# A two-layer encoder: the stage of seven products begins two groups earlier

## The chip, the cores and the metric

The kernel runs on one core of a Trainium2 chip. The metric is the time of one execution in microseconds (us) on the device, as the median of repeated runs; a profile was taken of one further execution. The engines are TensorE (PE, its weight loads PEld), VectorE (DVE), ScalarE (ACT), GpSimd (POOL) and SyncE (SP), whose queue issues all the transfers (DMA).

## The reference

Two layers of a streaming encoder over 1152 tokens (1024 of a prompt, 8 x 16 of samples), width 1024. In each layer an attention over a window and a causal convolution work side by side, one output projection joins them, and a feed-forward with a hidden width of 4096 follows. In the code, cut to what matters here:

```python
def finish_layer(x, attn_o, conv_o, beta_a, beta_c, w_out, g2, w_up, w_down):
    x = x + jnp.concatenate([attn_o * beta_a, conv_o * beta_c], axis=-1) @ w_out
    h = rms_norm(x, g2)
    return x + jnp.square(jax.nn.relu(h @ w_up)) @ w_down

for l in range(DEPTH):
    h = rms_norm(yp, norm1_g[l])
    q, k, v, u = project(h, w_in[l], q_norm_g[l], k_norm_g[l], pos_p)
    a_o = band_attention_prompt(q, k, v, attn_sinks[l])
    c_o = conv_tail(jnp.pad(u, ((0, 0), (CONV_STATE, 0), (0, 0))), conv_w[l], conv_b[l], conv_ln_g[l], conv_ln_b[l])
    yp = finish_layer(yp, a_o, c_o, beta_attn[l], beta_conv[l], w_out[l], norm2_g[l], w_up[l], w_down[l])
```

All is float32. The kernel multiplies in parts: each operand is split into a rounded high half and the rest, and three matmuls (high x high, high x rest, rest x high) make one product.

## The kernel before

The tokens lie in three blocks of 384 columns, numbered 0 to 2; the 1024 channels are eight tiles of 128 partitions. One product of a 1024-deep weight tile with a block is 8 x 3 = 24 matmuls of 128x384 (`gemm`, L213 to L215). Weights come as half units of 128x512: SyncE loads `raw`, ScalarE casts the high half into `w` (L205), GpSimd subtracts it for the rest (L206). There are four `raw` buffers (NRAW) and six `w` buffers (NW). Products end in one of three PSUM banks `g` (GB).

The feed-forward is cut into 16 groups of 256 hidden channels. For one block and one group it takes 4 x 12 matmuls up (two column tiles of the hidden layer, L213 to L215, then relu, square and a split by ScalarE and VectorE in `hidden`, L704 to L707) and 8 x 6 matmuls down (`down`, L723, each added to x by VectorE, L725). `feed_one` takes two groups at a time for one block, with 12 matmuls for each down bank. `feed_forward` with two blocks takes one group at a time for both, so that they share the weights.

For the last groups, blocks 0 and 1 go through a stage of seven products (`pair_feed`): a 2x2 partition of weights and activations by Strassen's scheme as Winograd has it, with seven products where eight stand in the plain form. One pass takes two groups: two `pair_up` (7 products of 12 matmuls each, L926) and one `pair_down` (2 x 7 x 12, L1006), 336 matmuls. It needs sums of weights (`S`, VectorE, L879), split by L892 and L893, and sums of the activations (`pair_forms`: differences `t` on GpSimd, L827, sums `m`, `c`, `r` on VectorE, L827, splits by L815 and L816), the last of which overwrite block 1's own `h`. The tiles `S`, `w` and `hid` of this stage lie in a pool `xp` that opens where the pools of the plain form (`hp` for the hidden tiles, `fp`, and the PSUM pool `aux`) close.

Work is interleaved when the program is written. `side` puts a generator on a lane (attention, convolution, forms), and `tick` moves each lane on at its rate; `back` holds one generator of feed-forward work, of which `unit_done` after each product of another stage takes `mix` steps (`fill`), and `flush` takes the rest. A scheduler then orders each engine's instructions by a model of time. `out(b)` is the output projection of block b (`w_out`, additions L695): it finishes the convolution (`tail_of`, whose end is conv_tail: L659, the two steps L249 and L255 of its norm, L670, L673, and L648 and L649, which write `co`), loads x[b] (L190) into one of the nine slots of the pool `big` (NS), and multiplies `ao` and `co` with eight column tiles of w_out.

Per layer: attention and convolution of the three blocks; `out(0)`; block 0's groups 0 to ALONE in the background; `out(1)`; block 1's groups 0 to ALONE; groups ALONE to PLACE for both blocks; then groups PLACE to PAIR for both in the background of `out(2)`; block 2's x is stored (`kept`), and groups PAIR to 16 go through the seven products. Block 2 runs all its groups by itself later.

## Time and profile before

| | |
|---|---|
| runs | 2385.42, 2387.70, 2388.78 us; median 2387.7 us |
| profiled execution | 2387.42 us, its span 2385.6 us |
| TensorE busy | 2312.7 us, 97% |
| VectorE, GpSimd, ScalarE busy | 70%, 63%, 53% |
| mean granted clock of TensorE | 0.995 of full speed |

The span goes from the first to the last instruction in the profile; the time of the execution has 1.8 us more around it. Busy is the share of the span in which an engine had an instruction under way. Matmuls overlap in TensorE's pipeline: one shows as 0.33 us, while the next starts after about half of that. So a busy share of TensorE says little of lost time, and counts of matmuls in a stretch say more.

### The profile page before, as it was taken

What the parts mean: (1) busy time and instruction counts of PE and PEld (TensorE: products, weight loads), DVE (VectorE), ACT (ScalarE), POOL (GpSimd) and SP (SyncE); (2) the same over time, 40 slices, a digit from 0 to 9 for tenths busy, and PEclk for the clock granted to TensorE, in tenths of its full rate; (3) what the DMA queues carried; (4) which work ended last, traced back from release to release, by engine and by line L of the source; (5) the groups of instructions that cost most, each with busy time, mean ns of one, the idle gap of its engine ahead of it and who ended that gap; (6) DMA issues with size and microseconds to landing.
All of it is one profiled execution on the core that took longest, in us unless ns stands there. A gap on an engine that the chain in (4) does not pass through costs nothing.

```text
span 2385.6 us, 39001 instructions
## 1 busy us (share of the span) xinstructions
PE 2312.7 (97%) x13822; PEld 2250.2 (94%) x13822; DVE 1676.6 (70%) x3153; ACT 1269.3 (53%) x2732; POOL 1514.6 (63%) x1247
## 2 busy tenths in 40 slices
PE   7999899999999999999999999999999999999999
PEld 7898898999989999999999999999999899999999
DVE  5999978996378777787687764799834877752222
ACT  5467546555335555644565566466433555544442
POOL 6975485656476665866856866856345666666662
PEclk9999999999999999999999999999999999999999
DMA  5423333434332223443334344434333122254442
GB/s 191 147 88 103 106 111 121 120 121 125 99 96 79 64 71 107 150 135 115 99 119 122 120 142 129 134 99 126 92 106 107 58 71 71 84 164 137 136 126 75
DMA packets 164260, 266.49 MB, mean 112 GB/s; under 512 B 24753, under 2 KB 55729, under 8 KB 164017
## 3 DMA queue, kind: packets, MB, share of 16 engines
q1 hardware_dynamic: 164064, 264.01, 35.8%
q8 instruction: 108, 1.77, 0.3%
q14 instruction: 88, 0.71, 0.1%
HBM read 250.19 MB, written 16.05 MB: 112 GB/s over the span
## 4 chain that ended last, share of the span: by engine, by line
PE 73%; DVE 18%; POOL 4%; issue 3%; DMA 2%; ACT 1%; DVEq 0%; POOLq 0%; SPq 0%; ACTq 0%
PE g L723 13%; PE g L213 12%; PE g L214 12%; PE g L215 12%; DVE c L355 6%; PE x L1006 4%; PE x L926 4%; PE g L1006 3%; PE m L723 2%; PE r L723 2%; PE g L926 2%; POOL w L893 2%; DMA A<-in_w 1%; PE c L723 1%; POOL w L206 1%
## 5 line engine op out<-in xcount | busy, mean ns | idle before, releaser
L206 POOL TENSOR_TENSOR w<-raw,w 128x512 fp32r<-128x512 f32 x728 | 972.7, 1347 | 599.5 <-ACT w L205 589.1
L205 ACT CAST w<-raw 128x512 fp32r<-128x512 f32 x728 | 445.1, 619 | 422.8 <-PE g L215 124.0
L213 PE MATMUL g<-h,w 128*128 128x384 f32 x1696 | 576.4, 341 | 8.2 <-ACT h L284 4.2
L214 PE MATMUL g<-h,w 128*128 128x384 f32 x1696 | 574.1, 339 | 0.6 <-DVE h L285 0.6
L215 PE MATMUL g<-h,w 128*128 128x384 f32 x1696 | 573.1, 338 | 0.0
L355 DVE SCALAR_TENSOR_TENSOR c<-u,vec,c 128x384 f32<-128x384 f32 (+1 forms) x960 | 498.0, 519 | 17.6
L723 PE MATMUL g<-hid,w 128*128 128x384 f32 x2304 | 429.1, 340 | 8.4 <-DVE x L725 5.3
L723 PEld LDWEIGHTS g<-hid,w 128*128 128x128 f32 x2304 | 397.8, 188 | 16.6 <-DVE x L725 9.5
L213 PEld LDWEIGHTS g<-h,w 128*128 128x128 f32 x1696 | 321.0, 189 | 12.4 <-ACT h L284 4.8
L214 PEld LDWEIGHTS g<-h,w 128*128 128x128 f32 x1696 | 321.0, 189 | 2.2 <-DVE h L285 1.0
L215 PEld LDWEIGHTS g<-h,w 128*128 128x128 f32 x1696 | 320.8, 189 | 0.9
L707 DVE TENSOR_TENSOR hid<-t,hid 128x384 fp32r<-128x384 f32 x128 | 107.5, 840 | 186.7 <-ACT hid L706 186.4
L893 POOL TENSOR_TENSOR w<-S,w 128x512 fp32r<-128x512 f32 x96 | 138.6, 1446 | 120.6 <-ACT w L892 120.3
L725 DVE TENSOR_TENSOR x<-x,g 128x384 f32<-128x384 f32 x240 | 130.0, 549 | 66.9 <-PE g L723 66.1
L704 ACT ACTIVATE t<-g 128x384 f32<-128x384 f32 x128 | 62.8, 491 | 148.2 <-PE g L215 147.7
L1006 PE MATMUL x<-F,w 128*128 128x384 f32 x624 | 120.4, 337 | 4.2 <-DVE x L1009 2.3
L893 POOL TENSOR_TENSOR w<-raw,w 128x512 fp32r<-128x512 f32 x64 | 90.5, 1414 | 41.9 <-ACT w L892 40.6
L1006 PEld LDWEIGHTS x<-F,w 128*128 128x128 f32 x624 | 109.3, 188 | 6.0 <-DVE x L947 2.5
L1006 PE MATMUL g<-F,w 128*128 128x384 f32 x528 | 107.6, 339 | 3.3 <-ACT F L815 1.4
L892 ACT CAST w<-S 128x512 fp32r<-128x512 f32 x96 | 59.7, 622 | 93.3 <-DVE S L879 48.2
L1006 PEld LDWEIGHTS g<-F,w 128*128 128x128 f32 x528 | 92.7, 188 | 7.1 <-ACT F L815 2.7
L893 POOL TENSOR_TENSOR w<-A,w 128x512 fp32r<-128x512 f32 x64 | 86.9, 1362 | 19.3 <-ACT w L892 19.1
(237 smaller groups left out, 4010.9 us busy)
## 6 DMA issues: line engine op xcount, KB each, us to landing
raw<-in_w SPq DMA_DIRECT2D x792, 256.0 KB, 2.7
A<-in_w SPq DMA_DIRECT2D x64, 256.0 KB, 2.7
x<-in_x SPq DMA_DIRECT2D x24, 384.0 KB, 5.0
x<-xd SPq DMA_DIRECT2D x12, 384.0 KB, 5.1
kept<-x SPq DMA_DIRECT2D x4, 768.0 KB, 4.0
x<-kept SPq DMA_DIRECT2D x8, 384.0 KB, 4.4
xd<-x SPq DMA_DIRECT2D x4, 768.0 KB, 4.9
out_y<-x SPq DMA_DIRECT2D x4, 768.0 KB, 4.4
```

The costliest lines, as they stand in the source:

```text
L205: nc.scalar.copy(u[:, 0], raw)
L206: nc.gpsimd.tensor_tensor(out=u[:, 1], in0=raw, in1=u[:, 0].bitcast(F32), op=ALU.subtract)
L213: nc.tensor.matmul(ps, lhsT=u(0, k), rhs=h(0, k), start=k == 0, stop=False)
L214: nc.tensor.matmul(ps, lhsT=u(0, k), rhs=h(1, k), start=False, stop=False)
L215: self.pe = nc.tensor.matmul(ps, lhsT=u(1, k), rhs=h(0, k), start=False, stop=k == KT - 1)
L355: t = nc.vector.scalar_tensor_tensor(out=o, in0=src(k), scalar=w, in1=o, op0=ALU.mult, op1=ALU.add)
L707: nc.vector.tensor_tensor(out=hid[:, 1], in0=f, in1=hid[:, 0].bitcast(F32), op=ALU.subtract)
L723: self.pe = nc.tensor.matmul(ps, lhsT=u(p), rhs=hid[:, q], start=i == 0, stop=i == n - 1)
L725: nc.vector.tensor_tensor(out=x[:, m], in0=x[:, m], in1=ps, op=ALU.add)
L893: nc.gpsimd.tensor_tensor(out=u[:, 1], in0=f[n], in1=u[:, 0].bitcast(F32), op=ALU.subtract)
L926: nc.tensor.matmul(ps, lhsT=u[:, p, k], rhs=H[h](q, k), start=start and k == 0 and i == 0, stop=k == 3 and i == 2, skip_group_check=True)
L1006: nc.tensor.matmul(o, lhsT=u[:, p, 2 * i + j], rhs=F(j, hn)[:, q], start=start and n == 0, stop=n == 5, skip_group_check=True)
```

## The change

Three tables are replaced by two. Before, layer 0 had ALONE 6, PLACE 7, PAIR 8, and layer 1 had 4, 6, 8. Now the seven products begin with group 6 in both layers (PAIR), five passes where there were four. Block 0 takes groups 0 to 6 by itself; block 1 takes 0 to 4 (FIRST) by itself and groups 4 and 5 around `out(2)`: its four products up stand ahead of the projection (`self.fill(4)`), its products down are its background. `feed_forward` with its two-block form is gone, and `feed_one` got the argument `then`, called between its last products up and down. FORMS, the rate at which the forms advance with each tick, was 0.3 and 0.2 and is 0.5.

```diff
-ALONE = (6, 4)
-PLACE = (7, 6)
-PAIR = (8, 8)
+PAIR = (6, 6)
+FIRST = (4, 4)
-FORMS = (0.3, 0.2)
+FORMS = 0.5
...
-    def feed_one(self, l, groups, block, pool=None):
+    def feed_one(self, l, groups, block, pool=None, then=None):
...
+            if then is not None and g == groups[-2]:
+                then()
             for m in range(KT):
...
-                self.back, self.mix = self.feed_forward(l, range(alone), [blk(0)]), mix[1]
+                self.back, self.mix = self.feed_one(l, range(pair), blk(0)), mix[1]
...
-                for _ in self.feed_forward(l, range(alone), [blk(1)], True):
-                    pass
-                for _ in self.feed_forward(l, range(alone, place), [blk(0), blk(1)]):
+                for _ in self.feed_one(l, range(first), blk(1)):
                     pass
...
-            self.back, self.mix = self.feed_forward(l, range(place, pair), [blk(b) for b in range(2)], then=firsts), mix[2]
+            self.back, self.mix = self.feed_one(l, range(first, pair), blk(1), then=firsts), mix[2]
+            self.fill(4)
             out(2)
```

Line numbers move: the products down at L723 stand at L722 in the changed kernel, their additions at L724, those of the projection at L694, the conv norm's L255 at L254, the sums `S` at L826, the weights' L206 at L205, and L827 at L774.

The first place is VectorE at the start of the seven products in layer 0. Before (x_4038 is block 1's x, x_7182 that of block 2, S the sums of weights):

```order
L725 TENSOR_TENSOR x_4038<-x_4038,g_7779 128x384
L725 TENSOR_TENSOR x_4038<-x_4038,g_7787 128x384
L725 TENSOR_TENSOR x_4038<-x_4038,g_7795 128x384
L695 TENSOR_TENSOR x_7182<-x_7182,g_7803 128x384
L725 TENSOR_TENSOR x_4038<-x_4038,g_7839 128x384
L725 TENSOR_TENSOR x_4038<-x_4038,g_7847 128x384
L725 TENSOR_TENSOR x_4038<-x_4038,g_7855 128x384
L725 TENSOR_TENSOR x_4038<-x_4038,g_7863 128x384
L879 TENSOR_TENSOR S_7890<-raw_7877,A_7879 128x512
L879 TENSOR_TENSOR S_7892<-S_7890,raw_7873 128x512
```

The same place of the changed kernel (x_6774 is block 2's x):

```order
L694 TENSOR_TENSOR x_6774<-x_6774,g_7069 128x384
L724 TENSOR_TENSOR x_4038<-x_4038,g_7110 128x384
L724 TENSOR_TENSOR x_4038<-x_4038,g_7129 128x384
L826 TENSOR_TENSOR S_7306<-raw_7293,A_7295 128x512
L694 TENSOR_TENSOR x_6774<-x_6774,g_7143 128x384
L826 TENSOR_TENSOR S_7308<-S_7306,raw_7289 128x512
L826 TENSOR_TENSOR raw_7293<-raw_7289,raw_7293 128x512
L826 TENSOR_TENSOR S_7418<-raw_7320,A_7322 128x512
L694 TENSOR_TENSOR x_6774<-x_6774,g_7179 128x384
```

The first sum stood behind the last addition of a product down and all additions of the projection; now four additions of the projection (g_7143, g_7179 and two more) stand behind it.

The second place is TensorE where block 2's convolution ends in layer 0 (r is the bank of the conv norm). Before, products down of block 1's groups 4 and 5 follow:

```order
L723 MATMUL g_6755<-hid_6671,w_6751 128x384 x2
L255 MATMUL r_6617<-cst,s_6625 128x128 x3
L723 MATMUL g_6755<-hid_6671,w_6751 128x384
L723 MATMUL g_6774<-hid_6561,w_6770 128x384 x3
L723 MATMUL g_6774<-hid_6611,w_6770 128x384 x3
L723 MATMUL g_6774<-hid_6671,w_6770 128x384 x3
```

Now (ao is the attention's output, so the last row belongs to the projection's second column tile; the first, g_6779, stands ahead of these rows):

```order
L722 MATMUL g_6856<-hid_6618,w_6852 128x384 x3
L254 MATMUL r_6624<-cst,s_6632 128x128 x3
L722 MATMUL g_6856<-hid_6696,w_6852 128x384 x3
L722 MATMUL g_6875<-hid_6568,w_6871 128x384 x3
L722 MATMUL g_6875<-hid_6618,w_6871 128x384 x3
L722 MATMUL g_6875<-hid_6696,w_6871 128x384 x2
L722 MATMUL g_6856<-hid_6750,w_6852 128x384
L722 MATMUL g_6875<-hid_6696,w_6871 128x384
L722 MATMUL g_6875<-hid_6750,w_6871 128x384
L722 MATMUL g_6856<-hid_6750,w_6852 128x384 x2
L722 MATMUL g_6875<-hid_6750,w_6871 128x384 x2
L212 MATMUL g_6897<-ao_4037,w_6899 128x384
```

Before, 384 more matmuls of groups 6 and 7 and the rest of the downs stood between the norm and most of the projection; now the projection begins around the norm.

The third place is GpSimd in the same stretch of the changed kernel (w are weight halves, t the differences for the forms, s the norm's power):

```order
L230 TENSOR_TENSOR s_6630<-s_6628,half 128x3
L205 TENSOR_TENSOR w_6899<-raw_6898,w_6899 128x512
L774 TENSOR_TENSOR t_6756<-h_5040,h_3255 128x384
L774 TENSOR_TENSOR t_6758<-h_5041,h_3256 128x384
L774 TENSOR_TENSOR t_6815<-h_5040,h_3255 128x384
L774 TENSOR_TENSOR t_6817<-h_5041,h_3256 128x384
L774 TENSOR_TENSOR t_6833<-h_5040,h_3255 128x384
L774 TENSOR_TENSOR t_6835<-h_5041,h_3256 128x384
L774 TENSOR_TENSOR t_6889<-h_5040 128x384
L205 TENSOR_TENSOR w_6904<-raw_6903,w_6904 128x512
L205 TENSOR_TENSOR w_6942<-raw_6941,w_6942 128x512
L774 TENSOR_TENSOR t_6891<-h_5041 128x384
```

The seven differences in a row stood before as well, between other weight halves; now the halves behind them are those of the first two tiles of the projection and of the products down beside them. In layer 1 three more differences follow in the same way.

## Rows read from the trace of the kernel before

**Rows 1.** The page, busy time of each engine.

```profile
PE 2312.7 (97%) x13822; PEld 2250.2 (94%) x13822; DVE 1676.6 (70%) x3153; ACT 1269.3 (53%) x2732; POOL 1514.6 (63%) x1247
```

**Rows 2.** The chain of waits: start us, length us, what.

```profile
609.70 16.66 PE g L723 x96
```

**Rows 3.** Windows: length; busy us and instructions per engine; granted clock; DMA share; GB/s.

```profile
575.30:693.60 118.30, 116.91 (x667) 115.02 (x666) 61.88 (x100) 47.48 (x88) 65.21 (x53) 1.00 0.33 103
693.60:760.80 67.20, 62.13 (x337) 59.53 (x336) 54.91 (x78) 34.57 (x69) 45.37 (x32) 0.97 0.25 79
760.80:823.00 62.20, 59.82 (x339) 58.54 (x338) 46.24 (x74) 32.69 (x65) 39.54 (x29) 1.00 0.22 68
823.00:880.70 57.70, 56.85 (x325) 56.44 (x324) 43.84 (x68) 31.69 (x63) 36.09 (x27) 1.00 0.23 71
...
1722.20:1861.10 138.90, 138.58 (x793) 137.19 (x793) 65.02 (x118) 53.40 (x99) 67.85 (x55) 1.00 0.30 95
1861.10:1925.50 64.40, 58.78 (x324) 56.24 (x325) 54.67 (x76) 34.36 (x69) 44.67 (x32) 1.00 0.24 74
...
1987.80:2045.60 57.80, 56.94 (x326) 56.52 (x326) 43.11 (x68) 31.70 (x63) 36.67 (x27) 1.00 0.24 71
```

**Rows 4.** Waits of TensorE, 693 to 719 us: us, times, longest.

```profile
PE x L926 <- POOL w L893: 1.8, 2, 0.9
PE x L926 <- ACT w L892: 1.7, 1, 1.7
PE x L926 <- DVE t L934: 1.3, 1, 1.3
```

**Rows 5.** Timeline of GpSimd at 700 us: start, length, what, [idle before].

```profile
699.68 1.74 POOL L893 TENSOR_TENSOR w<-S,w 128x512 fp32r<-128x512 f32 x1 [10.72 <-ACT w L892]
```

**Rows 6.** Timeline of VectorE, 697 to 702 us.

```profile
697.79 0.55 DVE L725 TENSOR_TENSOR x<-x,g 128x384 f32<-128x384 f32 x1 [0.49 <-PE g L723]
698.26 0.68 DVE L879 TENSOR_TENSOR S<-raw,A 128x512 f32<-128x512 f32 x1
...
700.19 1.78 DVE L879 TENSOR_TENSOR S<-raw,A 128x512 f32<-128x512 f32 x1
```

**Rows 7.** Timeline of VectorE at 1861 us.

```profile
1860.97 0.55 DVE L725 TENSOR_TENSOR x<-x,g 128x384 f32<-128x384 f32 x1
1861.44 0.69 DVE L879 TENSOR_TENSOR S<-raw,A 128x512 f32<-128x512 f32 x1
```

**Rows 8.** Timelines of TensorE and VectorE, end of the convolution in layer 0.

```profile
578.58 0.49 PE L255 MATMUL r<-cst,s 128*128 128x128 f32 x3
...
588.92 2.76 DVE L649 SCALAR_TENSOR_TENSOR co<-u,vec,co 128x384 fp32r<-128x384 f32 x2
```

**Rows 9.** Loads of x (L190), issue to landing.

```profile
DMA to landing us min/median/max: 3.4/5.0/7.3
```

**Rows 10.** Timeline of SyncE at 606 us.

```profile
605.94 0.90 SPq L190 DMA_DIRECT2D x<-in_x  x2
```

**Rows 11.** Waits of TensorE, 340 to 420 us, the longest.

```profile
PE g L214 <- DVE co L649: 1.4, 1, 1.4
```

**Rows 12.** Groups of GpSimd, 575.3 to 693.6 us: busy us, mean ns | idle before.

```profile
L206 POOL TENSOR_TENSOR w<-raw,w 128x512 fp32r<-128x512 f32 x36 | 48.3, 1356 | 47.2 <-ACT w L205 47.0
L827 POOL TENSOR_TENSOR t<-h 128x384 f32<-128x384 f32 x8 | 8.6, 1098 | 0.0
L827 POOL TENSOR_TENSOR t<-h,h 128x384 f32<-128x384 f32 x8 | 8.2, 1057 | 0.0
```

**Rows 13.** Groups of VectorE in the same stretch.

```profile
L827 DVE TENSOR_TENSOR m<-t,t 128x384 f32<-128x384 f32 x6 | 6.8, 1140 | 2.8 <-POOL t L827 2.8
...
L816 DVE TENSOR_TENSOR T<-m,T 128x384 fp32r<-128x384 f32 x4 | 2.2, 549 | 0.5 <-ACT T L815 0.5
```

**Rows 14.** A window in the same stretch, columns as in rows 3.

```profile
660.00:680.00 20.00, 18.61 (x102) 17.12 (x101) 18.36 (x32) 8.34 (x17) 20.00 (x18) 1.00 0.27 80
```

**Rows 15.** Waits of TensorE, 575 to 694 us, the longest.

```profile
PE g L723 <- DVE x L695: 0.9, 1, 0.9
```

More of the change, by code (lines that the diff above doesn't have):

```diff
@@ L754, in feed_one @@
                     yield
-    def feed_forward(self, l, groups, blocks, lag=False, pool=None, then=None):
-        a = self.a
-        if len(blocks) == 1:
-            yield from self.feed_one(l, groups, blocks[0], pool)
-            return
-        hids, ups, downs = {}, {}, {}
-        def up(e):
-            g, b = e
-            hids[e] = []
-            for j in range(2):
-                if (g, j) not in ups:
-                    ups[g, j] = self.unit(a["w"][l, 22 + 2 * g + j])
-                ps, _ = self.pg()
-                self.mark = self.gemm(ps, ups[g, j], blocks[b][1])
-                hids[e].append(self.hidden(ps))
-                self.tick()
-                yield
-        def down(e):
-            g, b = e
-            hid = hids.pop(e)
-            for j in range(2):
-                if (g, j) not in downs:
-                    downs[g, j] = self.unit(self.w_down(l, g)[:, ROW[g % 2 * 2 + j]::4], pool)
-            for m in range(KT):
-                self.down(blocks[b][0], m, [(lambda p, j=j: downs[g, j](p, m), hid[j]) for j in range(2)], pool)
-                if m % 4 == 3:
-                    if g == groups[-1]:
-                        self.stored(blocks[b], m, 4)
-                    self.tick()
-                    yield
-        es = [(g, b) for g in groups for b in range(len(blocks))]
-        if lag:
-            prev = None
-            for e in es:
-                yield from up(e)
-                if prev is not None:
-                    yield from down(prev)
-                prev = e
-            yield from down(prev)
-        else:
-            n = len(blocks)
-            for i in range(0, len(es), n):
-                for e in es[i:i + n]:
-                    yield from up(e)
-                if then is not None and i == len(es) - n:
-                    then()
-                for e in es[i:i + n]:
-                    yield from down(e)
     def parted(self, f, dst):
@@ L1041, in run @@
             nh = []
-            alone, pair, place, mix, conv, att = (t[l] for t in (ALONE, PAIR, PLACE, MIX, CONV, ATT))
+            pair, first, mix, conv, att = (t[l] for t in (PAIR, FIRST, MIX, CONV, ATT))
             def blk(b, end=False, x=x, h=h, nsrc=nsrc, nh=nh, l=l, fin=fin):
@@ L1098, in run @@
             forms, three, fourth = self.pair_forms(h[0], h[1])
-            self.side("forms", three, FORMS[l])
+            self.side("forms", three, FORMS)
             def firsts(l=l, fourth=fourth):
@@ L1141, in run @@
                 with tc.tile_pool(name=f"fp{l}", bufs=NFW) as fp:
-                    for _ in self.feed_forward(l, range(NG), [blk(2, True)], True, fp):
+                    for _ in self.feed_one(l, range(NG), blk(2, True), fp):
                         pass
             else:
-                self.back = self.feed_forward(l, range(NG), [blk(2, True)])
+                self.back = self.feed_one(l, range(NG), blk(2, True))
                 self.fill(FILL)
```

## The prediction

> **What bounds the kernel now.** The page comes first: TensorE is busy for 97% of the span, VectorE for 70%, GpSimd for 63% [rows 1]. So TensorE is the limit, and what remains to be found is the number of its matmuls and the places where it stands still. The chain of waits gives the price of a matmul: 96 in a row of the down product take 16.66 us, 0.1735 us each [rows 2]. Every matmul that the change touches has this form (128x384), so time lost in a stretch is its length less its count times 0.1735.
>
> The windows by stage [rows 3] then show three kinds of stretch. In the two from the last products up of block 1's first groups to the start of the seven products ("transition" from here on), 118.3 us hold 667 matmuls (115.7 us) in layer 0, and 138.9 us hold 793 (137.6 us) in layer 1: 2.6 and 1.3 us are lost. The first pass of the seven products takes 67.2 us for 337 matmuls and 64.4 us for 324: 8.7 and 8.2 us lost. The second and third passes take 62.2 us for 339 and 57.7 us for 325, so 3.4 and 1.2 us are lost, and in layer 1 the last row shows 57.8 us for 326, 1.2 us lost again. A pass counts 336 in the code; a window counts those that cross its edge twice.
>
> The wait view of the first pass says why it is dear [rows 4]: TensorE waits for weights from ScalarE and GpSimd (1.7 and 1.8 us), then for VectorE. Going back: GpSimd's first product weight that needs a sum begins at 699.68 us, after 10.72 us of idleness that ScalarE's cast ended [rows 5]; the cast waited for the sum; and VectorE made that sum at 698.26 us, directly behind the addition of the very last product down, at 697.79 us [rows 6]. Layer 1 repeats it: addition at 1860.97, first sum at 1861.44 us [rows 7]. In code the reason is plain: sums and weights of the stage lie in pool xp, which opens where the pool of the hidden tiles closes, so the last product down must have read them.
>
> **The change, part by part.**
>
> *Matmuls.* In each layer two groups of two blocks leave the plain form (2 blocks x 2 groups x 96 = 384 matmuls) and enter the seven products (336). That is 96 fewer in all: 96 x 0.1735 = 16.7 us off. They leave stretches in which TensorE is full, so this comes off the end.
>
> *One more pass per layer.* A pass loses between 1.2 and 3.4 us beyond its matmuls. In TensorE's order pass 3 of the changed kernel is interleaved exactly as pass 3 of before, passes 2 and 4 most nearly as pass 2, the dearer. So I take 3.4 us for the added one, 6.8 us in both layers (bounds 2.4 and 6.8).
>
> *The start of the seven products.* Now the last product down stands in front of four whole column tiles of the out projection: 4 x 24 x 0.1735 = 16.7 us. In VectorE's order the first sums come ahead of the additions of these four, so sums, casts and the weights that GpSimd splits have 16.7 us in which they cost nothing. The first pass should then lose what a later one loses, between 1.2 and 3.4, say 2.4 us: 8.7 + 8.2 - 4.8 = 12.1 us off. Bounds: nothing gained, if another wait takes the place of the sum, and 14.5 us, if both first passes fall to 1.2. If the cover were gone (the raw weights late behind the store of the third block, which heads SyncE's queue), the 12.1 us stay lost.
>
> *The transition, layer 0.* The out projection now begins only some ten products after the convolution's last step, and this has a price. From TensorE's broadcast (L255, 578.58 us) to VectorE's last split of co (591.68 us) the trace shows 13.1 us [rows 8]. The nine slots of the big pool (NS) are all taken, and the third block's x gets the one that the convolution's input gives up when co is done, so its load comes behind that: its landing takes 3.4 us at best and 5.0 us in the median [rows 9]; then 0.55 us for the addition. That frees the first bank 17.1 to 18.7 us after L255. The order puts 78 matmuls (6 + 12 + 12 + 12 + 24 + 12) between L255 and the product that needs that bank: 13.5 us. TensorE stands still for 3.6 to 5.2 us, part of it earlier on co itself. Before, the same load was issued at 605.94 us [rows 10], with plain products as cover. I take 4.6 us lost instead of 2.6: +2.0 us. The nearest case, out projection 1 of layer 0, where co is also just in time, shows a wait of 1.4 us for co [rows 11], which speaks for the lower end.
>
> *The transition, layer 1.* Here co is ready before the products up, and GpSimd is the risk. Ten differences for the sums of h stand with three weight halves in a row in its queue; at 1.08 and 1.36 us [rows 12] that is 14.9 us. GpSimd can be six weight tiles ahead (NW = 6, 12 matmuls each): 12.5 us. The rest, some 2.4 us, shows up on TensorE; what was lost before is partly the same kind. I take 2.8 us for 1.3: +1.5 us. Bounds: below, nothing lost in either transition (-3.9 us together); above, 5.2 us in layer 0, and in layer 1, if GpSimd has no lead at all when the differences begin, 14.9 less the 6.2 us that three halves give TensorE, 8.7 us.
>
> *Weights without sharing.* Block 0's and block 1's groups in layer 1 now load and split their own weights: 32 halves per two groups and two blocks where it was 16. A half gives TensorE 12 x 0.1735 = 2.08 us of work and costs GpSimd 1.36 us, so splitting hides; 0 us. The larger additions per bank (12 matmuls instead of 6) spare VectorE work off the path: 0 us.
>
> *Sum*, against the profiled execution's own 2387.42 us (the median of the runs shown is 2387.7, 0.3 above): -16.7 + 6.8 - 12.1 + 2.0 + 1.5 = -18.5, so 2368.9 us; as a median, 2369 us.
>
> One rule speaks against this. In rows 6 the same sum S<-raw,A takes 0.68 us at 698.26 and 1.78 us at 700.19 us, when GpSimd is splitting weights. The Trainium skill (SBUF — State Buffer, section Who interferes with whom) says that a VectorE instruction with two SBUF inputs and a GpSimd instruction that reads SBUF exclude each other, and that the later one waits for the whole of the other; the trace agrees with it in that row. By it the two engines' times in the transition would add up rather than overlap, which makes the slower rival below likelier than the sum alone does.
>
> **The rivals.**
>
> *The start stays dear* (12%). The sums are early, but a tile or a load is not: the first pass still loses 8 us. For it: SyncE's queue is in order, and a store of x stands before the last raw tiles. Against it: each of these loads has over 10 us before it is used. Sum: 2369 + 12.1 = 2381 us.
>
> *GpSimd and VectorE take turns* (5%); this one ends slower. In one transition GpSimd has 32 halves x 1.356 and 16 differences (8.2 + 8.6 us): 60.2 us [rows 12], against 384 x 0.1735 = 66.6 us of TensorE, where before it had 118 us. VectorE's part of the sums of h is 8 sums of two differences at 1.14 us [rows 13] and 32 operations at 0.55: 26.7 us. If these never overlap, a transition lasts 86.9 us, 20.3 more than TensorE needs; over both layers, less the 3.5 us allowed for, 2369 + 37 = 2406 us. It decides once more than some 15 us are lost in each transition. For it: GpSimd was full for 20.00 of 20 us in 660 to 680 us [rows 14]. Against it: there VectorE was busy for 18.36 of the same 20, and TensorE waited for VectorE only 0.9 us at its longest in the whole stretch [rows 15].
>
> *Half of that* (6%): 8 to 9 us lost more in each transition, 2386 us, no change to be seen.
>
> *Better than the sum* (10%): both first passes fall to 1.2 us, the added pass costs 1.2, the transitions lose nothing: -16.7 + 2.4 - 14.5 - 3.9 = -32.7; halfway there is 2362 us.
>
> **How the numbers follow.** The forecast has the remaining 67%: 2369 us, between 2364 (the first passes and layer 0's transition at their lower ends) and 2375 (both transitions at their upper bounds). The range 2361 to 2381 takes in the first rival and half of the last. Some 0.2% (4.8 us) is what a measurement of this kernel tells from no change. Forecast, better sum and first rival lie below 2382.9 us, the last of them narrowly: faster 0.88, the same 0.07, slower 0.05.
>
> **What would show it.** Five passes a layer, the middle three at 58 to 62 us. In the first pass, no granted clock below 1.00 (0.97 now [rows 3]) and its length near 60 us. The first sum S<-raw,A earlier than the last addition of the out projection. In layer 0's transition, waits for VectorE's co and for x, 4 to 5 us together, and in layer 1's, short waits for GpSimd's weights. I am wrong if the first pass keeps waits for GpSimd's product weights of microseconds, or if a transition loses more than 8 us.

## The result, and the profile after

The median of the changed kernel is 2374.3 us (2372.5 to 2378.0, four runs) against 2387.8 us: ratio 0.995, 95% interval 0.9934 to 0.9965. It is 13.5 us faster (8 to 16 by the interval), where 18.5 were forecast. The profiled execution took 2373.73 us, its span is 2371.7 us.

The first part of the page, to be read against [rows 1]: 96 matmuls fewer, and VectorE and GpSimd busier.

```profile
PE 2296.1 (97%) x13726; PEld 2235.5 (94%) x13726; DVE 1719.8 (73%) x3201; ACT 1300.9 (55%) x2796; POOL 1571.5 (66%) x1287
```

Next the windows by stage (length, busy us and instructions of PE, PEld, DVE, ACT, POOL, granted clock, DMA share, GB/s). All cuts from here on are at the same events in every kernel: the *plain stretch* runs from the last matmul of the third block's attention to the first of the seven products, and behind it comes the first pass. Nearly all matmuls there are 128x384, so that the loss is again the length less the count times 0.1735 us; the cuts make it uncertain by some 0.5 us. First before (its plain stretches reach further back than the transitions in [rows 3]):

```profile
523.00:693.60 170.60, 169.21 (x968) 166.78 (x968) 102.61 (x184) 75.08 (x144) 97.80 (x77) 1.00 0.37 115
1690.80:1861.10 170.30, 169.98 (x976) 168.28 (x975) 89.01 (x167) 66.54 (x128) 75.28 (x61) 1.00 0.29 93
```

The changed kernel, in layer 0 the plain stretch and the first four passes, in layer 1 the plain stretch and the first pass:

```profile
523.80:633.50 109.70, 106.06 (x595) 104.76 (x594) 86.65 (x150) 55.25 (x108) 84.98 (x65) 0.97 0.42 140
633.50:692.10 58.60, 55.53 (x315) 54.16 (x313) 44.30 (x67) 31.31 (x63) 37.02 (x28) 1.00 0.27 89
692.10:756.20 64.10, 61.83 (x350) 60.55 (x350) 47.85 (x78) 33.38 (x66) 39.86 (x29) 1.00 0.22 68
756.20:813.90 57.70, 56.85 (x325) 56.44 (x324) 43.89 (x68) 31.71 (x63) 36.29 (x27) 1.00 0.23 71
813.90:876.70 62.80, 61.52 (x350) 60.56 (x349) 47.46 (x76) 33.23 (x66) 39.43 (x29) 1.00 0.21 70
...
1685.00:1791.90 106.90, 103.97 (x595) 102.09 (x594) 75.03 (x118) 55.80 (x108) 83.75 (x65) 1.00 0.44 143
1791.90:1848.90 57.00, 55.10 (x314) 54.25 (x313) 42.52 (x67) 31.43 (x63) 36.08 (x27) 1.00 0.28 91
```

The first passes lose 3.9 and 2.5 us where they lost 8.7 and 8.2 [rows 3]. The plain stretches lose 109.7 - 595 x 0.1735 = 6.5 us and 3.7 us, where they lost 2.7 and 1.0. So the start gave 10.5 us, and more than half of that (6.5 us) was lost ahead of it. The waits of TensorE say on whom (us in total, times, longest); in the plain stretch of layer 0, of layer 1, and in layer 0's first pass:

```profile
PE g L212 <- DVE x L724: 2.2, 1, 2.2
PE g L722 <- DVE hid L706: 1.4, 1, 1.4
...
PE g L722 <- POOL w L205: 1.8, 1, 1.8
PE g L214 <- POOL w L205: 0.8, 1, 0.8
...
PE x L873 <- DVE t L881: 1.2, 1, 1.2
PE g L873 <- ACT t L877: 1.1, 1, 1.1
PE x L953 <- DVE x L956: 0.8, 1, 0.8
```

In the first pass, GpSimd's product weights, which cost 1.8 us before [rows 4], are gone from the list. In layer 1's plain stretch GpSimd's weights are there, as forecast. In layer 0's it is neither co nor the load of x, but a split of the hidden tile and an addition on VectorE. The timelines at that place, of GpSimd and of VectorE (start, us, instruction, idle time before it and its releaser):

```profile
579.20 6.46 POOL L774 TENSOR_TENSOR t<-h,h 128x384 f32<-128x384 f32 x6
...
581.21 1.37 DVE L774 TENSOR_TENSOR m<-t,t 128x384 f32<-128x384 f32 x1 [2.43 <-POOL t L774]
582.49 1.34 DVE L706 TENSOR_TENSOR hid<-t,hid 128x384 fp32r<-128x384 f32 x1
583.76 0.55 DVE L763 TENSOR_TENSOR T<-m,T 128x384 fp32r<-128x384 f32 x1
584.22 1.74 DVE L669 TENSOR_TENSOR u<-u,r 128x1536 f32<-128x1536 f32 x1
586.00 0.56 DVE L774 TENSOR_TENSOR r<-h,c 128x384 f32<-128x384 f32 x1
586.47 0.55 DVE L724 TENSOR_TENSOR x<-x,g 128x384 f32<-128x384 f32 x1
```

VectorE stands 2.43 us at a sum m whose differences GpSimd makes in a run of six; the hidden tile's split comes behind it, and the addition behind that, the convolution's L669 and more sums. TensorE waited 1.4 us for the split, until 583.9 us, and 2.2 us for the addition (the one at 586.47 us, which ends at 587.0, and TensorE goes on at 587.1). So the activations' sums are a suspect, and with them the weights that GpSimd splits for each block apart.

### The profile page after: what moved, and what is told of

It reads as the page before. It is cut to its first block, busy times and chain, and to the rows that moved or that the text cites. A ratio compares the mean times of both kernels' runs of the same rounds, so it can differ in the third digit from the quotient of the medians.

```text
span 2371.7 us, 39078 instructions
## 1 busy us (share of the span) xinstructions
PE 2296.1 (97%) x13726; PEld 2235.5 (94%) x13726; DVE 1719.8 (73%) x3201; ACT 1300.9 (55%) x2796; POOL 1571.5 (66%) x1287
## 5 line engine op out<-in xcount | busy, mean ns | idle before, releaser
L205 POOL TENSOR_TENSOR w<-raw,w 128x512 fp32r<-128x512 f32 x712 | 954.6, 1353 | 506.6 <-ACT w L204 495.2
L212 PE MATMUL g<-h,w 128*128 128x384 f32 x1568 | 532.1, 340 | 7.9 <-ACT h L283 3.9
L213 PE MATMUL g<-h,w 128*128 128x384 f32 x1568 | 530.1, 338 | 0.6 <-DVE h L284 0.6
L214 PE MATMUL g<-h,w 128*128 128x384 f32 x1568 | 529.1, 338 | 0.0
L722 PE MATMUL g<-hid,w 128*128 128x384 f32 x1920 | 363.6, 342 | 9.2 <-DVE x L724 4.1
L722 PEld LDWEIGHTS g<-hid,w 128*128 128x128 f32 x1920 | 333.5, 189 | 16.3 <-DVE x L724 5.4
L212 PEld LDWEIGHTS g<-h,w 128*128 128x128 f32 x1568 | 295.8, 189 | 12.3 <-ACT h L283 4.7
L213 PEld LDWEIGHTS g<-h,w 128*128 128x128 f32 x1568 | 296.0, 189 | 2.3 <-DVE h L284 1.0
L214 PEld LDWEIGHTS g<-h,w 128*128 128x128 f32 x1568 | 295.8, 189 | 0.9
L840 POOL TENSOR_TENSOR w<-S,w 128x512 fp32r<-128x512 f32 x120 | 168.8, 1409 | 129.1 <-ACT w L839 126.9
L953 PE MATMUL x<-F,w 128*128 128x384 f32 x780 | 151.2, 337 | 5.3 <-DVE x L956 3.4
L953 PEld LDWEIGHTS x<-F,w 128*128 128x128 f32 x780 | 136.8, 188 | 7.2 <-DVE x L956 4.7
L953 PE MATMUL g<-F,w 128*128 128x384 f32 x660 | 133.7, 338 | 0.9 <-DVE x L894 0.4
L953 PEld LDWEIGHTS g<-F,w 128*128 128x128 f32 x660 | 115.9, 188 | 3.8 <-DVE x L894 2.0
L956 DVE TENSOR_TENSOR x<-x,x 128x384 f32<-128x384 f32 x160 | 83.8, 545 | 47.7 <-PE x L953 47.2
```

Of the source, the lines that this page charges most:

```text
L205: nc.gpsimd.tensor_tensor(out=u[:, 1], in0=raw, in1=u[:, 0].bitcast(F32), op=ALU.subtract)
L212: nc.tensor.matmul(ps, lhsT=u(0, k), rhs=h(0, k), start=k == 0, stop=False)
L213: nc.tensor.matmul(ps, lhsT=u(0, k), rhs=h(1, k), start=False, stop=False)
L214: self.pe = nc.tensor.matmul(ps, lhsT=u(1, k), rhs=h(0, k), start=False, stop=k == KT - 1)
L722: self.pe = nc.tensor.matmul(ps, lhsT=u(p), rhs=hid[:, q], start=i == 0, stop=i == n - 1)
L840: nc.gpsimd.tensor_tensor(out=u[:, 1], in0=f[n], in1=u[:, 0].bitcast(F32), op=ALU.subtract)
```

## The experiments

**Theory A:** the start of the seven products is dear or cheap by where the last products down stand, and nothing else in the change touches it. The shortfall comes from GpSimd's and VectorE's work for the sums of the activations and for unshared weights, which lies beside fewer products than before. **Rivals:** the start is cheaper for another reason; the shortfall is the end of the convolution and the load of x (the forecast's own account), or only the order of the sums.

All losses below are worked out as above (us):

| kernel | median us | plain, layer 0 | first pass | plain, layer 1 | first pass |
|---|---|---|---|---|---|
| before | 2387.8 | 2.7 | 8.7 | 1.0 | 8.2 |
| changed | 2374.3 | 6.5 | 3.9 | 3.7 | 2.5 |
| e1, no early products up | 2392.0 | 9.0 | 6.8 | 8.5 | 8.3 |
| e2, before with early products | 2375.9 | 1.8 | 1.2 | 1.6 | 4.5 |
| e3, changed with four passes | 2381.5 | 4.1 | 3.8 | 3.9 | 2.1 |
| e4, convolution earlier | 2371.1 | 6.8 | 2.5 | 3.7 | 2.3 |
| e5, no sums of activations | 2362.7 | 0.7 | 1.1 | -0.5 | 1.7 |
| e6, differences on VectorE | 2380.7 | 11.8 | 2.1 | 4.2 | 2.1 |
| e7, e4 and sums spread | 2371.6 | 7.1 | 2.4 | 5.6 | 1.2 |
| e8, e4 and products down first | 2372.1 | 6.0 | 2.6 | 6.7 | 1.3 |
| e9, e4 and sums earlier | 2369.8 | 6.1 | 1.0 | 5.7 | 2.1 |
| e12, shared weights, five passes | 2375.1 | 7.1 | 1.3 | 2.2 | 1.4 |

**e1.** The products up run no longer ahead of the projection:

```diff
-            self.fill(4)
             out(2)
```

> The changed kernel without the early run of four products up: groups 4 and 5 of block 1 are interleaved with the third block's projection again, so the last product down ends right ahead of the seven products. Theory A (the start is cheap because four bare column tiles of the projection stand between the last product down and the first product of the seven): the first passes lose 8 to 9 us again instead of 4.0 and 2.5, +4.5 and +6; layer 0's transition has the products up as cover for the third block's x and gives back 2 to 4 of its 6.4 us. Together +6.5 to +10.5: 2381 to 2385 us, first passes of about 63 us in both layers. Rival B (the first passes are cheaper for another reason, the shorter plain stretch or the unshared weights, not for the place of the last products down): they stay at 57 to 58.6 us, and the time is 2370 to 2375 us.

It took 2392.0 us (2389.2 to 2396.5), ratio to before 1.002 (1.0011 to 1.0029): 17.7 us more than the changed kernel. In the windows the first passes are dear again, and the plain stretches lose more as well:

```profile
524.10:636.50 112.40, 105.36 (x596) 103.85 (x595) 78.80 (x145) 53.27 (x104) 76.08 (x61) 0.97 0.43 141
636.50:699.70 63.20, 58.58 (x325) 56.11 (x324) 53.73 (x76) 34.45 (x69) 45.36 (x32) 1.00 0.24 76
1691.70:1803.40 111.70, 105.83 (x595) 103.62 (x595) 74.33 (x116) 54.77 (x108) 78.99 (x63) 0.98 0.42 136
1803.40:1866.20 62.80, 56.04 (x314) 54.06 (x313) 48.37 (x69) 31.32 (x63) 41.35 (x30) 1.00 0.27 85
```

Theory A holds for the start (8.7 us more in the two first passes), and was wrong in that the plain stretch would be eased. The waits of layer 0's plain stretch tell why there:

```profile
PE g L212 <- ACT co L647: 4.9, 1, 4.9
PE r L254 <- DVE s L242: 2.2, 1, 2.2
```

The early products up cover the steps of the convolution's norm too. Without them co is waited for, 4.9 us, and the norm 2.2 us. (In layer 1 the longest wait is 2.8 us, for an addition on VectorE.) Without its one line the change would have been no gain.

**e2.** The kernel before, with one line more:

```diff
+            self.fill(8 if l else 4)
             out(2)
```

> The kernel before (seven products from group 8, four passes) with the products up, and in layer 0 the first down, of block 1's last groups run ahead of the third block's projection, so that bare column tiles of the projection stand ahead of the first pass. Theory A: the first pass of layer 0 falls from 67.2 us (8.7 lost) to about 61 (2.4 to 4 lost), 5 to 6 us off; in layer 1 the last product down still stands 12 matmuls ahead of the start, so there 0 to 2 us come off; the transition of layer 0 loses up to 2 us more. Together 2380 to 2384 us. Rival B (the place of the last products down is not what made the start dear): no difference, 2387 to 2389 us, first pass of layer 0 at 66 to 67 us.

It took 2375.9 us (2375.3 to 2376.5), ratio 0.995 (0.9939 to 0.9962). That is 11.9 us off, from the order alone, with the old number of matmuls:

```profile
523.60:695.40 171.80, 171.10 (x980) 168.90 (x979) 108.65 (x192) 77.36 (x149) 104.62 (x81) 1.00 0.35 114
695.40:751.10 55.70, 54.85 (x314) 54.28 (x313) 40.45 (x66) 31.33 (x63) 36.02 (x27) 1.00 0.28 93
1683.20:1847.90 164.70, 163.51 (x940) 162.14 (x940) 91.28 (x163) 66.00 (x128) 75.19 (x61) 1.00 0.29 92
1847.90:1915.20 67.30, 64.08 (x362) 62.64 (x361) 54.44 (x79) 34.27 (x69) 45.35 (x32) 1.00 0.26 83
```

Layer 0's first pass loses 1.2 instead of 8.7 us, layer 1's 4.5 instead of 8.2, and the plain stretches lose no more than before. That the start is cheaper for another reason than the place of the products is refuted; what I had expected of it (2380 us at best) was too little in both layers.

**e3.** The changed kernel with four passes:

```diff
-PAIR = (6, 6)
-FIRST = (4, 4)
+PAIR = (8, 8)
+FIRST = (6, 6)
```

> The changed kernel with four passes instead of five: seven products from group 8, block 1's groups 6 and 7 around the third block's projection, in the same order as the changed kernel has 4 and 5. Theory A (a pass more costs what the middle passes lose): 96 matmuls more (+16.7 us), one pass less per layer (-2.1 -2.3 to -3.4 -3.5), and layer 0's transition, where the convolution's end is then two groups further ahead of the projection, gives back 2 to 4 of its 6.4 us: +6 to +10, 2380 to 2384 us. Rival B (the matmuls taken out were not on the path, and all of the gain is the start of the seven products): 2372 to 2376 us, as the changed kernel. Rival C (the stall of layer 0's transition is not the convolution's end): no relief there, 6.4 us lost again, 2384 to 2387 us.

It took 2381.5 us (2380.2 to 2384.5), ratio 0.9977 (0.9968 to 0.9985): the fifth pass is worth 7.2 us, as theory A said. Set beside e2 it tells more. Both have 13822 matmuls, four passes and products ahead of the projection; e3 goes block by block and splits each weight twice. It differs in two more ways: its sums go at rate 0.5, and in layer 1 it has only the products up ahead of the projection, where e2 has the whole of group 6. It is 5.6 us slower. Its plain stretches of both layers, and the waits in either of them:

```profile
521.50:695.50 174.00, 171.63 (x979) 168.75 (x978) 104.42 (x175) 86.15 (x164) 126.37 (x97) 1.00 0.42 137
1687.00:1860.60 173.60, 171.23 (x978) 168.62 (x977) 89.42 (x143) 85.57 (x164) 125.03 (x97) 1.00 0.41 137
```

```profile
PE g L722 <- POOL w L205: 1.0, 2, 0.5
PE g L214 <- POOL w L205: 0.8, 1, 0.8
```

GpSimd is busy for 126 and 125 us, where e2's row shows 105 and 75, and TensorE waits 1.8 us in each layer for its weights (e2 waits for none in layer 0, and 1.2 us in layer 1). The losses there are 4.1 and 3.9 us against 1.8 and 1.6. With the first pass counted in, though, layer 1 loses 6.0 us in e3 and 6.1 in e2, and the whole difference lies in layer 0: 7.9 against 3.0.

**e4.** The third block's convolution in layer 0 a step faster:

```diff
-CONV = ((6, 5, 3), (3.5, 3.5, 3.5))
+CONV = ((6, 5, 4), (3.5, 3.5, 3.5))
```

> The changed kernel with the convolution of the third block in layer 0 moved on at a rate of 4 instead of 3, so that its last steps end earlier, ahead of the transition; layer 1 is as it was. Theory A (TensorE's 6.4 us in layer 0's transition are lost because the convolution's end, the forms' differences and the last products up fall together on VectorE and GpSimd): the transition loses 2 to 3.5 us, and the spell at half clock there is gone: 2370 to 2372 us. Rival B (the forms alone make the stall, a run of ten differences on GpSimd with VectorE's sums behind them): it stays at 5 to 7 us, 2373 to 2376 us.

It took 2371.1 us, ratio 0.9928 (0.9917 to 0.994, where the changed kernel's interval begins at 0.9934). The gain is not where theory A put it: the plain stretch of layer 0 loses 6.8 us, as much as before the edit. Rival B is right about the place and wrong about the time, since the gain lies ahead. The windows up to the plain stretch, of the changed kernel and of this one (its profiled execution was the fastest of its runs):

```profile
0.00:523.80 523.80, 483.98 (x3046) 459.70 (x3046) 463.21 (x979) 311.67 (x744) 346.87 (x317) 0.98 0.37 122
```

```profile
0.00:518.00 518.00, 481.93 (x3046) 459.19 (x3046) 457.97 (x977) 311.41 (x744) 347.25 (x317) 0.98 0.38 123
```

The same 3046 matmuls end 5.8 us earlier, beside the attention. But the run does not test the convolution's end: the projection came forward with it. From the norm's last step on TensorE (L254) to the first matmul on co there are 9.3 us in e4 and 14.4 in the changed kernel. Its place is tested by e5 and e8.

**e5.** The sums of the activations are left out; the seven products read h in their place.

```diff
-                "T1": part(T1), "T2": part(T2), "T4": part(T4)}, three(), fourth()
+                "T1": h1, "T2": lambda p, k: h1(p, 4 + k), "T4": h0}, iter(()), iter(())
```

> The changed kernel without the sums of the activations: the differences on GpSimd, the sums, splits and casts on VectorE and ScalarE are left out, and the seven products read plain halves of h in their place (so the output is not the reference's; TensorE's matmuls are the same). Theory A (the transitions lose what they lose because of these sums: VectorE in layer 0, GpSimd's queue in layer 1): layer 0's transition falls from 6.4 us lost to 1 to 3, layer 1's from 3.8 to 1 to 2, and the half-clock spell in layer 0's transition is gone; 2374 less 5 to 8 is 2366 to 2369 us. Rival B (the losses come from the convolution's end, the products up and the load of x, whatever the sums do): the transitions stay within 1 us of 6.4 and 3.8 us, 2372 to 2375 us.

```profile
531.90:635.80 103.90, 103.55 (x595) 102.34 (x595) 65.43 (x113) 49.97 (x94) 66.61 (x50) 1.00 0.42 137
1681.50:1784.10 102.60, 102.60 (x594) 102.30 (x593) 52.82 (x79) 49.50 (x94) 66.90 (x50) 1.00 0.42 139
```

Both plain stretches are full: 0.7 us lost and none, at full clock, though in layer 0 the convolution's end (8.4 us from the norm's last step to the first matmul on co) and the load of x are still there, and in both layers the weights without sharing. So without the sums nothing else in the stretch stalls TensorE. The median, 2362.7 us, is not a clean price, because the kernel without the sums' tiles differs elsewhere too (its first 300 us hold 1649 matmuls, the changed kernel's 1700); only these windows are used. Nor does e5 say what the convolution's end costs beside the sums, since it has no sums. The same groups of VectorE by form show how the sums act on what stands beside them, the split of the hidden tile in the plain stretch of layer 0, with the sums (changed) and without (e5):

```profile
L706 DVE TENSOR_TENSOR hid<-t,hid 128x384 fp32r<-128x384 f32 x8 | 7.2, 901 | 2.1 <-ACT hid L705 2.1
```

```profile
L706 DVE TENSOR_TENSOR hid<-t,hid 128x384 fp32r<-128x384 f32 x8 | 5.6, 702 | 2.5 <-ACT hid L705 2.5
```

One takes 901 ns with GpSimd busy for 85.0 us of the stretch, 702 ns with 66.6. The Trainium skill (SBUF — State Buffer, Who interferes with whom) has VectorE instructions with two inputs in SBUF, as this split is, and GpSimd's reads of SBUF exclude each other; the rows agree in direction.

**e6.** The 16 differences of a layer on VectorE:

```diff
-            d = op(nc.gpsimd, self.tmp(), F(h1, 0, k), F(h, 0, j), sub)
-            e = op(nc.gpsimd, self.tmp(), F(h1, 1, k), F(h, 1, j), sub)
+            d = op(nc.vector, self.tmp(), F(h1, 0, k), F(h, 0, j), sub)
+            e = op(nc.vector, self.tmp(), F(h1, 1, k), F(h, 1, j), sub)
```

> The changed kernel with the differences for the sums of the activations (16 in each layer) on VectorE instead of GpSimd. Theory A (in layer 1 GpSimd's queue is what TensorE waits for, in layer 0 VectorE's, which stands behind GpSimd's differences): layer 1's transition falls from 3.8 us lost to 1.5 to 2.5 and shows no wait for GpSimd's weights; in layer 0 VectorE gets 10 to 16 operations of 0.55 to 1.1 us more but no longer waits 2.4 us for GpSimd, so 5 to 8 us are lost there. Together 2371 to 2376 us. Rival B (VectorE is the tight one in both): both transitions lose 2 to 5 us more, 2378 to 2384 us.

It took 2380.7 us (2375.1 to 2381.9), ratio 0.9965 (0.9952 to 0.9977). The plain stretch of layer 0:

```profile
524.90:639.90 115.00, 107.04 (x595) 104.60 (x594) 98.00 (x168) 55.34 (x109) 68.22 (x49) 0.97 0.41 133
```

In layer 0 the loss goes from 6.5 to 11.8 us: VectorE is the tight one there, busy for 98 of 115 us. In layer 1 it stays at 4.2, but no wait for GpSimd's weights is left; the longest are now for an addition on VectorE (1.3 us) and for a cast on ScalarE (1.2 us). Neither theory was right in whole: the time is rival B's, layer 1 lies between the two.

**e7, e8, e9.** Three other orders, each on top of e4. The sums spread over the products up:

```diff
-FORMS = 0.5
+FORMS = 1
```

> The changed kernel with the third block's convolution at rate 4 in layer 0 and the sums of the activations moved on at rate 1 instead of 0.5 with each product, so that they are spread over the four products up and do not come in one run behind the last of them; it is to be compared with the kernel that has the convolution's rate alone (2371.1 us). Theory A (the run of sums in one piece makes the stalls in both layers): layer 0's transition loses 2 to 4 us, layer 1's 1.5 to 3; 2365 to 2369 us. Rival B (it is their amount against 66.6 us of products, not where they stand): within 2 us of 2371.

Two steps of products down, too, ahead of the projection:

```diff
-            self.fill(4)
+            self.fill(6)
```

> The changed kernel with the third block's convolution at rate 4 in layer 0 and two steps more of block 1's products down (of the four in a transition) ahead of the third block's projection, so that six instead of four of its column tiles stand bare ahead of the seven products; to be compared with the kernel that has the convolution's rate alone (2371.1 us). Theory A (what stalls in layer 0 is the first tiles of the projection, behind the convolution's end and the load of x; the products down ahead of it are cover): layer 0's transition falls from some 6 us lost to 3 to 5, the first passes stay within 1 us; 2367 to 2371 us. Rival B (the additions of the products down stand in VectorE's queue behind the sums, wherever the projection stands): the transition loses as much or up to 3 us more; 2371 to 2375 us.

The sums begun two groups of block 1 earlier:

```diff
-FIRST = (4, 4)
+FIRST = (2, 2)
...
-            self.fill(4)
+            self.fill(12)
```

> The changed kernel with the third block's convolution at rate 4 in layer 0, and with the sums of the activations begun one stretch of two groups earlier in both layers: eight of a layer's 16 differences then lie beside block 1's groups 2 and 3 and only the other eight beside the transition; TensorE's order is nearly that of the kernel with the convolution's rate alone (2371.1 us), to which it is to be compared. Theory A (it is the amount of sums beside the 66.6 us of the transition's products that stalls, on GpSimd and with it on VectorE): the transitions lose 2 to 4 us less in each layer, and the half-clock spell in layer 0's is gone: 2363 to 2368 us. Rival B (the sums stall TensorE wherever they stand, since their operations hold VectorE and GpSimd in turn; the loss moves to block 1's groups 2 and 3): 2370 to 2373 us. Rival C (what remains in layer 0 is the convolution's end and the load of x): layer 1 gains 2 to 3 us, layer 0 nothing: 2368 to 2370 us.

They took 2371.6, 2372.1 and 2369.8 us (intervals 0.9921 to 0.9944, 0.9922 to 0.9946 and 0.9908 to 0.9935). None can be told from e4, so rival B holds in e7 and e8. In e8 the projection begins 9.1 us behind the norm's last step, where it begins 3.1 us ahead of it in the changed kernel, and layer 0 still loses 6.0 us: a projection too near to the convolution's end is not the main cause. The time of e9 lies between rivals B and C; by the place it is B, since layer 1 gains nothing (5.7 us lost, 3.7 in e4). TensorE's longest wait in layer 0's plain stretch now ends at 546.1 us, in the groups ahead of the transition:

```profile
PE g L722 <- DVE x L724: 1.8, 1, 1.8
```

The plain stretches lose 6.1 and 5.7 us with half the sums some 33 us earlier: what the transition gained, the groups ahead of it lost. Over e4 and these three, layer 0 loses 6.0 to 7.1 us and layer 1 3.7 to 6.7, wherever the sums stand.

**e10, e11.** A sixth pass, in layer 1 alone (with the early sums in layer 0), and in both layers:

```diff
-PAIR = (6, 6)
-FIRST = (4, 4)
+PAIR = (6, 4)
+FIRST = (2, 2)
...
-            self.fill(4)
+            self.fill(4 if l else 12)
```

> The kernel with the sums begun earlier in layer 0 (as the one before), and in layer 1 the seven products from group 4 instead of 6, so one pass more there (48 matmuls fewer, 8.3 us), with the sums beside the transition. Theory A (a further pass pays its matmuls less 2.5 to 3.5 us, as the fifth did): 5 us off the layer; against it, the attention of the third block now has two groups of products fewer beside it, 1 to 4 us lost: within -5 to +1 of the kernel with the early sums, less the 2 to 3 us that early sums give in layer 1, so 2363 to 2370 us. Rival B (attention, convolution and sums no longer fit beside what is left of the products): 2372 to 2380 us.

```diff
-PAIR = (6, 6)
-FIRST = (4, 4)
+PAIR = (4, 4)
+FIRST = (2, 2)
...
-CONV = ((6, 5, 3), (3.5, 3.5, 3.5))
+CONV = ((6, 5, 6), (3.5, 3.5, 3.5))
```

> The changed kernel with the seven products from group 4 in both layers, six passes instead of five (96 matmuls fewer, 16.7 us), the third block's convolution in layer 0 at rate 6 so that it ends in time, and the sums beside the transition. Theory A (each pass more pays 8.3 us of matmuls less 2.5 to 3.5): 10 us less than the 2371 to 2374 us of the changed kernel, less 2 to 6 us of losses because the attention, the convolution and the sums have fewer products beside them: 2364 to 2370 us. Rival B (these no longer fit): losses of 10 us or more in each layer, 2375 to 2385 us.

They took 2399.3 and 2457.8 us (ratios 1.0047, 1.0034 to 1.0059, and 1.0292, 1.0278 to 1.0306): both misses, rival B in kind and worse in size. Layer 1's plain stretch in e10, its longest waits, and the place in layer 0 of e11 where the convolution is finished:

```profile
1672.90:1759.50 86.60, 59.26 (x301) 56.18 (x302) 62.74 (x117) 31.47 (x61) 41.23 (x32) 0.81 0.29 98
...
PE r L658 <- DVE T L763: 10.5, 1, 10.5
PE g L212 <- ACT co L647: 6.2, 1, 6.2
PE r L248 <- DVE f L665: 5.1, 1, 5.1
```

```profile
510.00:578.00 68.00, 18.52 (x65) 14.97 (x66) 43.70 (x102) 18.89 (x56) 9.27 (x12) 0.50 0.10 35
...
PE r L658 <- DVE f L655: 34.7, 1, 34.7
```

34 us are lost in e10 (86.6 - 301 x 0.1735): the convolution's end and its norm wait for VectorE with nothing beside them. A part of the first wait is of another kind: L658's operand was ready at 1697.4 us, but it writes the bank r, of which the kernel has one at this place, and a sum of the activations held that until VectorE had split it at 1704.7 us. The plain products are the cover for the third block's attention and convolution, and the seven products, which come behind, can't be. As these stages stand, with that one bank for both, neither try at a sixth pass paid; a second bank was not tried.

**e12.** Five passes in the form of before, where blocks 0 and 1 share the weights of the last plain groups:

```diff
-ALONE = (6, 4)
-PLACE = (7, 6)
-PAIR = (8, 8)
+ALONE = (4, 4)
+PLACE = (5, 5)
+PAIR = (6, 6)
...
-FORMS = (0.3, 0.2)
+FORMS = (0.5, 0.5)
...
+            self.fill(4)
             out(2)
```

> The kernel before with the seven products from group 6 in both layers (five passes, as many matmuls as the changed kernel), the products up of blocks 0 and 1 for group 5 ahead of the third block's projection, and the sums of the activations at rate 0.5; so it differs from the changed kernel in that both blocks go through their last plain groups together and share these weights (block 0 has four groups by itself instead of six). Theory A (the weights without sharing, costed at nothing, are a price: with four passes the form by blocks lost 5.6 us against the shared form, 2381.5 to 2375.9): half the groups' weight splits leave GpSimd's queue in the transition, which loses 2 to 3 us less in each layer; 2367 to 2371 us. Rival B (sharing is worth nothing here, and those 5.6 us were the rate of the sums or the place of the projection): 2373 to 2377 us. Rival C (block 0's two groups less beside the third block's attention leave that stage uncovered in layer 1): a loss of 3 to 10 us ahead of the transition there, 2374 to 2382 us.

It took 2375.1 us (2372.5 to 2377.6), ratio 0.9951 (0.9938 to 0.9965): the changed kernel's time, rival B's. The windows say it is not that sharing is worth nothing. Up to layer 0's plain stretch, and the two plain stretches:

```profile
0.00:517.70 517.70, 479.21 (x2990) 453.93 (x2991) 455.72 (x963) 309.01 (x740) 338.61 (x311) 0.97 0.37 120
517.70:637.70 120.00, 116.45 (x651) 112.90 (x651) 99.43 (x183) 49.66 (x99) 69.78 (x56) 0.99 0.33 106
1687.20:1792.10 104.90, 104.08 (x592) 101.68 (x592) 76.07 (x133) 47.05 (x93) 62.04 (x49) 1.00 0.32 106
```

In layer 1 the plain stretch and first pass lose 3.6 us together, where the changed kernel loses 6.2; GpSimd has 62 us of work there, not 84. In layer 0 GpSimd has 70 us and the stretch still loses 7.1: there sharing doesn't help, which fits e6, as VectorE is no less busy there than in the changed kernel (99.4 of 120.0 us, 86.7 of 109.7). And ahead of layer 0's stretch 56 matmuls fewer than in the changed kernel (9.7 us) end only 6.1 us earlier: the two groups of block 0 that are gone were cover, as rival C has it, but in the other layer. What sharing alone is worth with five passes stays open, since no run here gives it without that loss.

## Why the prediction came out as it did

The sign, the mechanism of the start and the order of size were right; the sum was 5 us too good. In its own terms, read from the windows: the start gave 10.5 us instead of 12.1, the two added passes cost 4.4 instead of 6.8, and the plain stretches lose 6.5 us more than before, where the two transitions were to lose 3.5 more. With the matmuls that makes -16.3 us; the two profiled executions differ by 13.7, and the rest lies outside these windows or at their edges, with no cause found. Three runs split the 13.5 us into steps, each the difference of two medians:

| step | forecast | measured |
|---|---|---|
| products up early, before to e2 | -12.1 | -11.9 |
| blocks apart, weights not shared, e2 to e3 | 0 | +5.6 |
| one more pass per layer, e3 to the changed kernel | -16.7 + 6.8 = -9.9 | -7.2 |
| the two transitions | +2.0 + 1.5 | in the two steps above |

The steps also say that e2, the old form with one line more, can't be told from the whole change: its runs (2375.3 to 2376.5 us) lie inside those of the changed kernel (2372.5 to 2378.0). Most of what the fifth pass gains, the step to blocks apart had lost.

*Start.* Right, and shown by e1 and e2 from both sides. The first sums came early, no product weight of GpSimd was waited for in layer 0's first pass, and its clock stayed at 1.00. The rival that the start stays dear is refuted.

*Weights without sharing: the term put at nothing.* I costed it at 0, since a half's split (1.36 us) is shorter than its products (2.08 us). That holds for splitting alone: e5 splits the same halves and loses 0.7 us in layer 0 and none in layer 1. Beside the sums, GpSimd has differences to make in the same queue, and in e3 TensorE waits 1.8 us in each layer for w; e2 has the sums and loses under 2 us in each plain stretch. So the two together are the likely cause of the step's 5.6 us, of which the forecast had put 1.5 into layer 1's transition. They are not shown to be the whole: e2 and e3 differ in the sums' rate as well (a further rise in e7 gave nothing) and in layer 1's order, and with the first pass counted in only layer 0 loses more.

*Matmuls and the added pass.* 96 matmuls came off by the count. The added pass in layer 0 costs 2.1 us: passes 2 to 4 lose 3.4, 1.3 and 2.1 us, where before 2 and 3 lost 3.4 and 1.3 (57.7 us for 325 matmuls in [rows 3]; the forecast has 1.2 there). In layer 1 it costs 2.3 (64.2 us for 350, 57.7 for 325 and 63.0 for 350, against 62.3 for 339 and 57.8 for 326). So that term was too dear by 2.4 us in all. Against it, layer 0's plain stretch loses 2.4 us more with five passes (e3's 4.1 to 6.5): the sums then have 595 matmuls beside them instead of 979, and the convolution's end stands near the projection again (14.4 us from the norm's last step to the first matmul on co, 66.6 in e3); no run parts the two. Another 2.3 us lie ahead of that stretch, which begins at 523.8 us and in e3 at 521.5; their cause is open. With 0.3 us from layer 1's plain stretch and the first passes, that makes -7.3, near the -7.2 of the medians.

*Transition, layer 0.* In the window I priced 6.4 us are lost, where 4.6 were forecast and 5.2 was the upper bound, and the cause was wrong:

```profile
574.40:633.50 59.10, 55.45 (x304) 54.69 (x303) 46.14 (x73) 28.32 (x53) 52.61 (x41) 0.94 0.43 143
```

No wait of TensorE for co or for the third block's x is in the list; e5 kept the convolution's end and the load and lost 0.7. It is VectorE with the sums: behind GpSimd's differences here, and with more work of its own in e6. The two waits are 3.6 us; most of the rest is that TensorE ran at half clock behind them, as the last section shows. The account of co is not false in itself: take the early products up away, as e1 does, and it costs 4.9 us.

*Transition, layer 1.* GpSimd's queue, as forecast: 3.7 us lost where 2.8 were forecast, 2.6 of them in waits for its weights. Moving the differences away (e6) shifted the waits to VectorE and ScalarE and gave back nothing.

*The rival that GpSimd and VectorE take turns* is refuted as a whole by its own sign, more than some 15 us lost in each transition: it is 6.5 and 3.7 us for the whole plain stretches. (The busy times would not show it, 86.65 and 84.98 us in 109.7: an instruction that is stretched counts as busy for its whole length, as the sum of 1.78 us in [rows 6].) What is left of it is the stretched split of e5's rows.

## What to carry to other kernels

Ahead of a stage that needs prepared operands, put the last work that these wait for in front of work that is independent of them: one line did that here and was worth 11.9 us in the kernel before and 17.7 in the changed one. A side task that hides by itself (here a weight split, 1.36 us under 2.08 us of products) is to be priced together with everything else in the same engine's queue in that stretch; here the two together are the likely price of 5.6 us. And before a cheaper form takes over more of the work, ask which stages used the dearer form as their cover: the fifth pass paid 7 us, the sixth cost 28 us or more, as built here.

## What the runs showed of the hardware

TensorE's clock fell to half after pauses that are short. In the changed kernel it was idle for 1.4 us until 583.9 and for 2.2 us until 587.1 us, with four matmuls between; for 6.8 us from 585.8 on the granted clock was 0.50, the 1.2 GHz level:

```profile
585.80:592.60 6.80, 5.53 (x17) 5.53 (x18) 6.21 (x12) 6.60 (x14) 6.80 (x6) 0.50 0.26 79
```

The 17 matmuls were under way for 5.53 us, 2.6 us more than 17 x 0.1735. And the same place of the program does not always lead to it. In layer 0's last pass TensorE stands still for 1.8 us, in the changed kernel (until 910.6 us) and in e4 (until 903.7); behind it the changed kernel ran on at full clock, e4 at half for 3.4 us:

```profile
911.00:918.00 7.00, 7.00 (x42) 7.00 (x41) 6.69 (x14) 5.71 (x13) 3.43 (x4) 1.00 0.14 50
```

```profile
904.70:908.10 3.40, 3.40 (x12) 3.40 (x12) 2.85 (x7) 2.46 (x7) 0.00 (x0) 0.50 0.02 5
```

The spell in e4 costs some 1.3 us (3.4 - 12 x 0.1735), more than half of the 2.3 us by which the medians of e4, e7, e8 and e9 differ at most, so single profiles of these can't be ranked by their spans. In e11 the clock stayed at half through the whole 68 us in which TensorE had 65 matmuls.
